# One masked copy per block instead of two in the windowed attention of a two-layer decoder trunk, with the difference of the values as the second operand

## The chip, the cores and the metric

One core of a Trainium2 chip runs the whole program. The metric is the device time of one execution in microseconds (us). Three runs of the kernel before took 986.33, 987.54 and 988.58 us; their median is 987.54 us.

The engines that matter are TensorE (PE in the profile; PEld are its weight loads), VectorE (DVE), ScalarE (ACT), GpSimd (POOL) and SyncE (SP, which issues nearly all DMAs). Each works through its own instructions in program order and waits at an instruction until semaphores of the others allow it.

## The reference

The trunk has two layers over 1024 positions of width 1024. Layer 0 is a gated pooling mixer and isn't touched. Layer 1 is gated attention with 16 heads of width 64, two key/value heads, a sink per head, a position bias, and a window of 128 positions. In blocks of 128 queries it is:

```python
def block_fn(args):
    qn, kn, vn, mn = args            # kn, vn: the previous and the own block, 256 keys
    s = jnp.einsum('bqhgd,bkhd->bhgqk', qn, kn).astype(jnp.float32) + pos_bias
    s = jnp.where(mn[None, None, None], s, NEG_INF)
    m = jnp.maximum(jnp.max(s, axis=-1, keepdims=True), sink)
    p = jnp.exp(s - m)
    p = p / (jnp.sum(p, axis=-1, keepdims=True) + jnp.exp(sink - m))
    return jnp.einsum('bhgqk,bkhd->bqhgd', p.astype(vn.dtype), vn)
...
o = o.transpose(1, 0, 2, 3, 4, 5).reshape(B, S, B_WIDTH)
return (o * jax.nn.silu(z)) @ w_out
```

The mask lets query i of a block see key j of the previous block for j > i, and key j of its own block for j <= i. For a given place j of the 128, a query so sees exactly one of the two keys.

## The kernel before

The activations lie with the channel on the partitions and the positions along a row. Every operand of a matmul is split into a high and a low part, so a product takes three matmuls (L203, L204, L205 in `dense_mm`: weights `wh`, `wl` against both parts of the activations). The weights are loaded by SP into `raw` and split there and then by `split_w` (L121 on ACT, L123 on DVE).

Layer 1 is one list of steps, `specs` (L1332), in two halves `q` of 512 positions. For each half and each of four groups `r` of four heads there are two steps `queries`, then `start`, then two steps `gates`; between them stand `keys`, `values` and `values_split` of the second half, the preparation of the activations of later steps (`Modulated.step`: L177 on DVE, L159 and L163 on ACT, L167 on POOL), and the output projections. `start` puts four blocks `attend(q, r, b)` on a list of events with due times, in units of an estimated PE time; the order of PE is written out by it (`manual_schedule` for PE alone, L1355). The other engines of layer 1 have their instructions ordered by a scheduler of the framework, which is why their order can shift when instructions are added.

One `attend` has three parts. First the scores go into a bank of PSUM (L1097, L1098); since a place j belongs to one key only, the scores of the two blocks are merged there by a predicated copy with the triangle `tri` (L1099), so that a block has 128 scores for a query instead of 256; bias, minimum and exponential follow (L1103 on DVE, L1107 on ACT), then the reciprocal and the scaling (L1110, L1111 on DVE). Some microseconds later PE transposes the probabilities into the bank "tp" (L1117), and ACT and DVE split them into `cur` (L1120, L1121). A `cur` holds probabilities that belong partly to keys of the previous block and partly to keys of the own one. For a block with b > 0, POOL makes the masked copy `prev` (L1126, what belongs to the previous block, the rest zero) and then masks `cur` in place (L1129). After a further pause PE multiplies the values of the previous block by `prev` and those of the own block by `cur` into bank "o" (L1140, L1141, two matmuls each). There are 28 such blocks; the four with b = 0 have no previous block.

Bank "o" exists once. It is emptied by ACT into the tile `ol` (L1143) and by DVE, which adds the two halves (L1147, twice); gate and split follow (L1151, L1152, L1153).

The values come from `values(q)`: ACT copies the projection out of PSUM into the tile `vt` (L1025). `values_split(q)` (L1030) transposes it on PE into a bank "d" (L1034), and splits it there into `VS` (L1037 on ACT, L1038 on DVE): `VS` has for each of 16 slots (block times key/value head) a high and a low part of 64 columns each. `vt` and `ol` share the tag "ol" of the pool `bp`, with one buffer: a new tile of that tag gets it only when every reader of the tile before is done. The first `values_split` stands behind the first `queries` of the half q = 0, the second behind the first `queries` of its third group.

Of the kernel before, what the change touches and what calls it, by code (L numbers as in the profile page):

```python
# [12 lines left out]
F32 = mybir.dt.float32  # L13
F32R = mybir.dt.float32r
AF = mybir.ActivationFunctionType
ALU = mybir.AluOpType
PSUM = bass.MemoryType.PSUM

P = 128
D = 1024  # L20
T = 1024
H = 512
# [33 lines left out]
def trunk(ctx, tc, xT, c, pack, ada_first, ada_rest, wu0_in, wg0_in, wa, wg, wao, wkv,  # L56
          wb, wbo, bias_in, outT):
    nc = tc.nc
# [7 lines left out]
    pp = ctx.enter_context(tc.tile_pool(name="psum", bufs=1, space=PSUM))  # L66
# [3 lines left out]
    def bank(tag):  # L70
        return pp.tile([P, H], F32, tag=tag, name="ps_" + tag, bufs=BANKS[tag])
# [146 lines left out]
    with ExitStack() as sa:  # L218
# [111 lines left out]
        blk, blk_k = {}, {}  # L330
# [467 lines left out]
        with tc.manual_schedule(engines={ET.PE}):  # L798
            nxt = pair_w(*steps[0])
            for i, (kind, g, j) in enumerate(steps):  # L800
                w, nxt = nxt, pair_w(*steps[i + 1]) if i + 1 < len(steps) else None
                if kind == "U":
                    parts = []
# [172 lines left out]
        with tc.manual_schedule(engines={ET.PE, ET.Activation, ET.DVE, ET.Pool}):  # L976
            for _, _, f, args in sorted(plan, key=lambda e: e[:2]):
# [3 lines left out]
    bp = ctx.enter_context(tc.tile_pool(name="bpool", bufs=1))  # L981
# [6 lines left out]
                            channel_multiplier=1, compare_op=ALU.is_ge, fill=0)  # L988
# [2 lines left out]

    VS = bp.tile([P, 16, 2, 64], F32R, name="VS")

# [23 lines left out]
    vts = {}  # L1020
# [9 lines left out]
    def values_split(q):  # L1030
        def run(w):
            ps = bank("d")
            for j in range(4):
                nc.tensor.transpose(ps[:, j * P:(j + 1) * P], vts[q][:, j * P:(j + 1) * P], ident)  # L1034
            pv = ps.rearrange("p (s c) -> p s c", c=64)
            vh, vl = VS[:, q * 8:q * 8 + 8, 0, :], VS[:, q * 8:q * 8 + 8, 1, :]
            nc.scalar.copy(out=vh, in_=pv)  # L1037
            nc.vector.tensor_sub(out=vl, in0=pv, in1=vh.bitcast(F32))  # L1038
            yield 0.43
        return None, run  # L1040

# [36 lines left out]
    def attend(q, r, b):  # L1078
        kv = r // 2
# [6 lines left out]
                              in_=nsink[:, 4 * r:4 * r + 4].unsqueeze(2))  # L1086
        nm = sp.tile([P, 4], F32, tag="nm", name="nm")
        den = sp.tile([P, 4], F32, tag="den", name="den")
        for j in range(2):
            s = bank("S").rearrange("p (e c) -> p e c", e=2)  # L1090
            lo = 0 if b else P
# [8 lines left out]
            for e in range(2):  # L1100
# [3 lines left out]
                    out=pt[:, i, :P], in0=s[:, e, :P], in1=bias[:, hd, :],  # L1104
# [7 lines left out]
                             in1=den.unsqueeze(2).broadcast_to([P, 4, P]))  # L1112
# [6 lines left out]
        cur = bp.tile([P, 2, H], F32R, tag="ph", name="cur", bufs=2)  # L1119
        nc.scalar.copy(out=cur[:, 0], in_=tp)  # L1120
        nc.vector.tensor_sub(out=cur[:, 1], in0=tp, in1=cur[:, 0].bitcast(F32))  # L1121
        parts = [(b, cur)]
        if b:
            prev = bp.tile([P, 2, H], F32R, tag="pp", name="prev", bufs=1)
            v8 = lambda t: t.rearrange("p x (a i) -> p (x a) i", i=P)
            nc.gpsimd.affine_select(out=v8(prev), in_=v8(cur).bitcast(F32),  # L1126
                                    pattern=[[0, 8], [-1, P]], base=-1, channel_multiplier=1,
                                    compare_op=ALU.is_ge, fill=0.0)
            nc.gpsimd.affine_select(out=v8(cur), in_=v8(cur).bitcast(F32),  # L1129
                                    pattern=[[0, 8], [1, P]], base=0, channel_multiplier=-1,  # L1130
                                    compare_op=ALU.is_ge, fill=0.0)
            parts = [(b - 1, prev), (b, cur)]
        yield LAGS[1]
        while (q, r) not in szs:
            yield KSTEP
        sz = szs[q, r]
        o = bank("o")
        for x, (blk, ph) in enumerate(parts):
            v = VS[:, 2 * blk + kv].rearrange("p x c -> p (x c)")
            mm(o, v, ph[:, 0], start=x == 0, stop=False)  # L1140
            mm(o, v, ph[:, 1], start=False, stop=x == len(parts) - 1)  # L1141
        ol = bp.tile([P, H], F32, tag="ol", name="ol", bufs=1)
# [2 lines left out]
        for e in range(2):  # L1145
            es = slice(e * 2 * P, (e + 1) * 2 * P)
            nc.vector.scalar_tensor_tensor(  # L1147
                out=of[e * 64:(e + 1) * 64, :], in0=o[0:64, es], scalar=0.5,
                in1=ol[0:64, es], op0=ALU.mult, op1=ALU.add)
# [4 lines left out]
                             in1=qt[:, :, 0, cols].bitcast(F32))  # L1154
# [132 lines left out]
    def start(q, r, gap):  # L1287
        def f():
            t = max(clock[0] + FIRST, last_start[0] + gap)
            for b in range(4):  # L1290
                push(t + gap * b, attend(q, r, 4 * q + b))
            last_start[0] = t + gap * 3
        return bare(f)
# [130 lines left out]
```

## Time and profile before

The profiled execution took 987.29 us, its span from the first to the last instruction 985.4 us, at a mean granted PE clock of 0.998.

| engine | busy, us | share of the span | instructions |
|---|---|---|---|
| PE | 962.5 | 98% | 4538 |
| DVE | 776.1 | 79% | 1411 |
| ACT | 458.6 | 47% | 902 |
| POOL | 143.8 | 15% | 173 |

Matmuls overlap in the profile: a 128x512 one is shown with about 390 ns, while one starts every 0.22 to 0.23 us. So a busy PE says that it never lacked work, not that it is at its peak, and its real losses are the rows in which it waits. A row of a timeline gives the start, the duration, the engine, the line of the kernel, the operation, output and inputs, and how many instructions are merged; where an engine was idle before, a bracket gives the idle time and the instruction that ended it. A row of the waits gives who waited for whom, the total, the number of times and the longest.

### The profile page before, as it was taken

To read this page: it belongs to the slowest core of one execution; us is meant where nothing else is said; L and a number is where in the kernel's file an instruction comes from. 1 tells how busy PE (TensorE), PEld (TensorE's weight loads), DVE (VectorE), ACT (ScalarE), POOL (GpSimd) and SP (SyncE) were. 2 spreads that over 40 slices of the span, in tenths; PEclk is the share of its full clock that TensorE was granted. 3 is DMA by queue.
4 is the path that set the end of the run, shared out by engine and by line. 5 is a ranking of instruction groups with operands and counts; after the bars stand their busy time and mean duration, and the time that the engine had idled before them with its cause. 6 is when DMAs were issued, how large, how long until landed. Compare 5 with 4: busy or idle time off the path is not lost.

```text
span 985.4 us, 12696 instructions
## 1 busy us (share of the span) xinstructions
PE 962.5 (98%) x4538; PEld 800.6 (81%) x4538; DVE 776.1 (79%) x1411; ACT 458.6 (47%) x902; POOL 143.8 (15%) x173
## 2 busy tenths in 40 slices
PE   8999999999999999999999998999999999999996
PEld 6788888888888887888888886877788888887786
DVE  5997978687978698677772268599899878889995
ACT  6533435333433244551111235486677555656534
POOL 2100000000000000000000000053334213336723
PEclk9999999999999999999999999999999999999999
DMA  9453621254125412789861212312221221123222
GB/s 332 182 171 124 192 91 65 88 190 159 55 99 189 157 48 76 245 300 329 303 200 55 74 64 101 114 65 65 79 71 65 87 86 65 64 85 109 86 87 85
DMA packets 40625, 125.67 MB, mean 128 GB/s; under 512 B 4465, under 2 KB 6641, under 8 KB 40434
## 3 DMA queue, kind: packets, MB, share of 16 engines
q1 hardware_dynamic: 40416, 123.82, 36.8%
q10 hardware_dynamic: 146, 1.05, 0.3%
q8 instruction: 35, 0.57, 0.2%
q14 instruction: 28, 0.23, 0.1%
HBM read 111.22 MB, written 13.63 MB: 127 GB/s over the span
## 4 chain that ended last, share of the span: by engine, by line
PE 73%; DVE 18%; ACT 3%; issue 3%; POOL 1%; DMA 1%; SPq 0%; POOLq 0%; DVEq 0%; ACTq 0%
PE ps_d L214 13%; PE ps_d L635 9%; PE ps_S L214 8%; PE ps_d L205 6%; PE ps_d L203 6%; PE ps_d L204 6%; PE ps_S L635 4%; PE ps_o L214 4%; PE ps_tp L214 3%; DVE wl L123 3%; PE ps_tp L635 2%; PE ps_o L635 2%; DVE tmp L541 2%; PE ps_d L374 2%; PE ps_tp L1117 1%
## 5 line engine op out<-in xcount | busy, mean ns | idle before, releaser
L121 ACT CAST wh<-raw 128x1024 fp32r<-128x1024 f32 x80 | 83.7, 1047 | 110.4 <-PE ps_d L214 78.0
L123 DVE TENSOR_TENSOR wl<-raw,wh 128x1024 fp32r<-128x1024 f32 x80 | 102.8, 1285 | 37.0 <-ACT wh L121 33.1
L203 PE MATMUL ps_d<-hm,wh 128*128 128x512 f32 x288 | 114.0, 396 | 1.1 <-ACT wh L121 1.1
L205 PE MATMUL ps_d<-hm,wl 128*128 128x512 f32 x288 | 112.7, 391 | 1.4 <-DVE wl L123 1.4
L204 PE MATMUL ps_d<-hm,wh 128*128 128x512 f32 x288 | 112.5, 391 | 0.0
L239 DVE CUSTOM_DVE_ANT_0 tmp<-tmp,cact,pk 128x1024 f32<-128x1024 f32 x48 | 60.6, 1282 | 29.6 <-DMA tmp<-ada_rest 29.5
L214 PE MATMUL ps_d<-gh,wh 128*128 128x512 f32 x224 | 82.0, 389 | 0.0
L205 PEld LDWEIGHTS ps_d<-hm,wl 128*128 128x128 f32 x288 | 54.1, 188 | 14.4 <-DVE wl L123 3.0
L214 PE MATMUL ps_S<-gh,wh 128*128 128x512 f32 x192 | 64.5, 390 | 0.0
L203 PEld LDWEIGHTS ps_d<-hm,wh 128*128 128x128 f32 x288 | 54.2, 188 | 11.7 <-ACT wh L121 1.5
L635 PE MATMUL ps_d<-hs,ws 128*128 128x512 f32 x264 | 63.4, 389 | 0.0
L1107 ACT ACTIVATE pt<-pt,nm 128x129 f32<-128x129 f32 x128 | 50.1, 394 | 26.8 <-DVE nm L1103 24.6
L204 PEld LDWEIGHTS ps_d<-hm,wh 128*128 128x128 f32 x288 | 54.2, 188 | 9.9
L635 PEld LDWEIGHTS ps_d<-hs,ws 128*128 128x128 f32 x264 | 49.6, 188 | 10.3
L541 DVE TENSOR_TENSOR tmp<-tmp 128x1039 f32<-128x1039 f32 (+3 forms) x40 | 49.4, 1235 | 6.8 <-ACT tmp L671 5.7
L611 ACT CAST ws<-tw 128x512 fp32r<-128x512 f32 x44 | 26.8, 621 | 54.5 <-PE ps_tp L214 15.1
L635 PE MATMUL ps_d<-ha,ws 128*128 128x512 f32 x216 | 51.9, 389 | 0.0
L533 POOL MEMSET tmp<- 128x16 f32 x16 | 1.7, 111 | 331.0 <-DVE tmp L541 116.2
L214 PEld LDWEIGHTS ps_d<-gh,wh 128*128 128x128 f32 x224 | 42.0, 188 | 8.7
L635 PEld LDWEIGHTS ps_d<-ha,ws 128*128 128x128 f32 x216 | 40.6, 188 | 8.4
L214 PE MATMUL ps_d<-gh,wl 128*128 128x512 f32 x112 | 43.6, 389 | 0.0
L147 POOL TENSOR_TENSOR rs<-v,mhalf 128x4 f32<-128x4 f32 (+1 forms) x7 | 7.1, 1018 | 239.7 <-DVE v L145 239.7
(292 smaller groups left out, 2477.0 us busy)
## 6 DMA issues: line engine op xcount, KB each, us to landing
tmp<-ada_rest SPq DMA_DIRECT2D x48, 512.0 KB, 4.5
raw<-wb SPq DMA_DIRECT2D x32, 512.0 KB, 3.3
raw<-wa SPq DMA_DIRECT2D x28, 512.0 KB, 3.5
raw<-wao SPq DMA_DIRECT2D x20, 512.0 KB, 3.7
ad<-ada_first SPq DMA_DIRECT2D x16, 512.0 KB, 4.9
x<-xT SPq DMA_DIRECT2D x32, 256.0 KB, 5.8
raw<-wbo SPq DMA_DIRECT2D x16, 512.0 KB, 3.3
kept_g<-tmp SPq DMA_DIRECT2D x14, 512.0 KB, 2.9
```

The costliest lines, as they stand in the source:

```text
L121: nc.scalar.copy(out=wh, in_=raw)
L123: nc.vector.tensor_sub(out=wl, in0=raw, in1=wh.bitcast(F32))
L203: mm(ps, lh, acts(k, 0), start=k == 0, stop=False)
L204: mm(ps, lh, acts(k, 1), start=False, stop=False)
L205: mm(ps, ll, acts(k, 0), start=False, stop=k == n - 1)
L214: mm(p, lhs, acts(k, hl, q), start=start and k == 0 and s == 0, stop=stop and k == n - 1 and s == 2)
L239: nc.vector.tensor_tensor_reduce(out=raw, in0=raw, in1=ca, scale=0.5, scalar=pk[:, bcol:bcol + 1], op0=ALU.mult, op1=ALU.add, accum_out=ad ...
L374: mm(psu[i, q], w0[k // 2][:, k % 2, w, i * P:(i + 1) * P], block(k, q)[hl], start=k == 0 and s == 0, stop=k == KT - 1 and s == 2)
L541: nc.vector.tensor_add(out=nx[:, 2 * s - 1:], in0=cur[:, 2 * s - 1:], in1=cur[:, s - 1:PAD + T - s])
L611: nc.scalar.copy(out=ws[i][:, 0, :], in_=src)
L635: mm(ps, lhs, acts(k, hl), start=start and k == 0 and s == 0, stop=k == 3 and s == 2, skip_group_check=True)
L1107: nc.scalar.activation(pt[:, i, :P + 1], pt[:, i, :P + 1], AF.Exp, bias=nm[:, i:i + 1], scale=-1.0, accum_out=den[:, i:i + 1])
```

## The change

`VS` stays. A second tile `DS` holds, in the same layout, the difference of the values: own block minus previous block. A block with b > 0 now multiplies the unmasked probabilities `cur` by the values of the previous block, and one masked copy `own` (what belongs to the own block) by the difference; the sum is the same. `cur` is not masked any more, and the copy `prev` is gone. `values_split` makes `DS`: it copies the transposed values back into `vt` (ACT), subtracts the previous block's values in place in the PSUM bank (DVE), and splits the result (ACT, DVE). The last block of the first half is kept in `v_last` for the second half.

```diff
     VS = bp.tile([P, 16, 2, 64], F32R, name="VS")
 
+    DS = bp.tile([P, 16, 2, 64], F32R, name="DS")
+    v_last = bp.tile([P, 2, 64], F32, name="v_last")
...
             nc.scalar.copy(out=vh, in_=pv)
             nc.vector.tensor_sub(out=vl, in0=pv, in1=vh.bitcast(F32))
+            vf = vts[q].rearrange("p (s c) -> p s c", c=64)
+            nc.scalar.copy(out=vf, in_=pv)
+            lo = 0 if q else 2
+            dh, dl = DS[:, q * 8 + lo:q * 8 + 8, 0, :], DS[:, q * 8 + lo:q * 8 + 8, 1, :]
+            if q:
+                nc.vector.tensor_sub(out=pv[:, 0:2, :], in0=pv[:, 0:2, :], in1=v_last)
+            else:
+                nc.scalar.copy(out=v_last, in_=vf[:, 6:8, :])
+            nc.vector.tensor_sub(out=pv[:, 2:8, :], in0=pv[:, 2:8, :], in1=vf[:, 0:6, :])
+            nc.scalar.copy(out=dh, in_=pv[:, lo:, :])
+            nc.vector.tensor_sub(out=dl, in0=pv[:, lo:, :], in1=dh.bitcast(F32))
             yield 0.43
...
-        parts = [(b, cur)]
+        parts = [(VS, b, cur)]
         if b:
-            prev = bp.tile([P, 2, H], F32R, tag="pp", name="prev", bufs=1)
+            own = bp.tile([P, 2, H], F32R, tag="pp", name="own", bufs=1)
             v8 = lambda t: t.rearrange("p x (a i) -> p (x a) i", i=P)
-            nc.gpsimd.affine_select(out=v8(prev), in_=v8(cur).bitcast(F32),
-                                    pattern=[[0, 8], [-1, P]], base=-1, channel_multiplier=1,
-                                    compare_op=ALU.is_ge, fill=0.0)
-            nc.gpsimd.affine_select(out=v8(cur), in_=v8(cur).bitcast(F32),
+            nc.gpsimd.affine_select(out=v8(own), in_=v8(cur).bitcast(F32),
                                     pattern=[[0, 8], [1, P]], base=0, channel_multiplier=-1,
                                     compare_op=ALU.is_ge, fill=0.0)
-            parts = [(b - 1, prev), (b, cur)]
+            parts = [(VS, b - 1, cur), (DS, b, own)]
...
-        for x, (blk, ph) in enumerate(parts):
-            v = VS[:, 2 * blk + kv].rearrange("p x c -> p (x c)")
+        for x, (vs, blk, ph) in enumerate(parts):
+            v = vs[:, 2 * blk + kv].rearrange("p x c -> p (x c)")
```

Lines behind the insertion have other numbers in the changed kernel; in its rows below L1040 and L1041 are the split into `VS` (L1037, L1038 before), L1043 the copy into `vt`, L1047 and L1050 the subtractions, L1051 and L1052 the split into `DS`, L1068 and L1069 the split of the queries (L1054, L1055), L1121 the exponential (L1107), L1156 `ol` (L1143), L1160 to L1166 the steps behind it (L1147 to L1153), L1142 the masked copy, L1099 the small copy of POOL (L1085).

The order of PE has the same rows at the same places, with `cur` and `own` in place of `prev` and `cur`. The first place that changes otherwise is POOL's, at the first two blocks with b > 0. Before:

```order
L1085 COPY pt<-nsink 128x4
L167 TENSOR_TENSOR hm<-xn,hm 128x512
L1126 AFFINE_SELECT prev<-cur 128x1024
L1129 AFFINE_SELECT cur<-cur 128x1024
L167 TENSOR_TENSOR hm<-xn,hm 128x512 x2
L1085 COPY pt<-nsink 128x4
L1126 AFFINE_SELECT prev<-cur 128x1024
L167 TENSOR_TENSOR hm<-xn,hm 128x512
L1129 AFFINE_SELECT cur<-cur 128x1024
```

Now:

```order
L1099 COPY pt<-nsink 128x4
L167 TENSOR_TENSOR hm<-xn,hm 128x512
L1142 AFFINE_SELECT own<-cur 128x1024
L167 TENSOR_TENSOR hm<-xn,hm 128x512 x2
L1099 COPY pt<-nsink 128x4
L1142 AFFINE_SELECT own<-cur 128x1024
L167 TENSOR_TENSOR hm<-xn,hm 128x512 x3
```

The second masked copy is gone, and L167 follows the first at once. The second place is ACT's, at the second `values_split`. Before:

```order
L1107 ACTIVATE pt,den<-pt,nm 128x129 x3
L1143 ACTIVATE ol<-ps_o 64x512
L1107 ACTIVATE pt,den<-pt,nm 128x129
L1054 ACTIVATE qt<-ps_d 64x512
L1037 CAST VS<-ps_d 128x8x64
L121 CAST wh<-raw 128x1024
L1152 CAST qt<-of 128x2x128
L1054 ACTIVATE qt<-ps_d 64x512
L159 ACTIVATE hm<-xn,adac,acol 128x512 x2
L1143 ACTIVATE ol<-ps_o 64x512
L163 ACTIVATE xn<-xn,adac,acol 128x512
```

Now, with what each instruction waits for (the engine whose semaphore it is):

```order
L1121 ACTIVATE pt,den<-pt,nm 128x129 [waits DVE_49] x3
L1068 ACTIVATE qt<-ps_d 64x512 [waits PE_49]
L1040 CAST VS<-ps_d 128x8x64 [waits PE_49]
L121 CAST wh<-raw 128x1024 [waits DMAHW5_49]
L1068 ACTIVATE qt<-ps_d 64x512 [waits DVE_49]
L1043 COPY vt<-ps_d 128x512 [waits DVE_49]
L159 ACTIVATE hm<-xn,adac,acol 128x512 x2
L163 ACTIVATE xn<-xn,adac,acol 128x512 [waits Activation_49]
L1156 ACTIVATE ol<-ps_o 64x512 [waits DVE_49]
L1051 CAST DS<-ps_d 128x8x64
```

The first of the two `ol` has moved from between the exponentials to behind the copy into `vt`, two L159 and an L163, and waits for DVE. The third place is DVE's at the same point. Now:

```order
L1124 RECIPROCAL den<-den 128x4
L1125 TENSOR_TENSOR pt<-pt,den 128x4x128
L1069 SCALAR_TENSOR_TENSOR qt<-ps_d,qt 64x512
L1041 TENSOR_TENSOR VS<-ps_d,VS 128x8x64
L123 TENSOR_TENSOR wl<-raw,wh 128x1024
L1069 SCALAR_TENSOR_TENSOR qt<-ps_d,qt 64x512
L1047 TENSOR_TENSOR ps_d<-ps_d,v_last 128x128
L1050 TENSOR_TENSOR ps_d<-ps_d,vt 128x384
L1160 SCALAR_TENSOR_TENSOR of<-ps_o,ol 64x256 x2
L1052 TENSOR_TENSOR DS<-ps_d,DS 128x8x64
L1164 TENSOR_TENSOR of<-of,szb 128x256
L177 TENSOR_TENSOR xn<-x,rb_4924 128x512
```

Before, the two L1147 (L1160 here) stood ahead of the reciprocal (L1110, L1124 here); now they stand behind the two subtractions. Two L177 that stood further back in the program now stand among the steps behind them.

## The prediction

> **What bounds the kernel now.** I read the page first for the span, then the waits of TensorE (PE), then the busy time by stretches, then the timelines of the engines where PE waits.
>
> ```profile
> span 985.4 us, 12696 instructions
> ```
>
> The profiled execution took 987.29 us, so 1.9 us lie outside the span. The change touches only layer 1, from about 620 us on. The busy time there, by stretches (start and end; span; then PE, weight load, DVE, ACT and POOL, each with its count):
>
> ```profile
> 640.00:710.00 70.00, 65.86 (x327) 54.32 (x327) 65.76 (x153) 54.24 (x122) 29.29 (x26) 1.00 0.19 61
> 710.00:740.00 30.00, 29.92 (x156) 25.21 (x155) 27.87 (x69) 20.79 (x49) 9.25 (x10) 1.00 0.26 88
> 740.00:900.00 160.00, 160.00 (x799) 135.06 (x798) 136.12 (x345) 95.92 (x238) 51.56 (x54) 1.00 0.23 76
> 900.00:940.00 40.00, 37.20 (x192) 30.46 (x191) 37.71 (x87) 24.05 (x62) 28.77 (x22) 1.00 0.27 92
> ```
>
> From 740 to 900 us PE never pauses: whatever delays PE before that is paid in full, and whatever DVE or POOL save there is worth nothing. PE is idle for 4.1 us in 640 to 710 and for 2.8 us in 900 to 940, the two places where DVE is 94% busy. What it waits for in all of layer 1:
>
> ```profile
> PE ps_tp L1117 <- DVE pt L1111: 6.1, 5, 1.6
> ```
>
> That is the probabilities of a block, the last DVE step before PE transposes them. No row has PE waiting for a masked copy (L1126, L1129). So the removal can earn only through DVE, and at most those 6.1 us and the 0.34 us of L205 below. The places (start, duration; the last bracket is PE's idle time and its releaser), with two rows where it does not wait now:
>
> ```profile
> 659.67 0.63 PE L1117 MATMUL ps_tp<-ident,pt 128*128 128x128 f32 x4 [1.60 <-DVE pt L1111]
> ...
> 694.24 0.60 PE L1034 MATMUL ps_d<-ident,vt 128*128 128x128 f32 x4
> ...
> 698.80 0.39 PE L1140 MATMUL ps_o<-prev,VS 128*128 128x512 f32 x1
> ...
> 708.89 0.50 PE L205 MATMUL ps_d<-hm,wl 128*128 128x512 f32 x1 [0.34 <-DVE wl L123]
> ...
> 903.98 0.63 PE L1117 MATMUL ps_tp<-ident,pt 128*128 128x128 f32 x4 [1.52 <-DVE pt L1111]
> ```
>
> **The change, part by part: what it removes.** PE issues the same matmuls in the same order with other operands, so its own work is unchanged. POOL loses one of two masked copies in 28 blocks (count, total, mean in ns):
>
> ```profile
> L1129 POOL TENSOR_SCALAR_AFFINE_SELECT cur<-cur 128x1024 fp32r<-128x1024 f32 x28 | 32.5, 1160 | 1.8
> ```
>
> 32.5 us of POOL go, but POOL is idle most of the time, and PE reads its copy several us after it is made. What can count is that DVE runs longer while POOL works. POOL, then DVE, at two of the waits:
>
> ```profile
> 655.28 1.16 POOL L1129 TENSOR_SCALAR_AFFINE_SELECT cur<-cur 128x1024 fp32r<-128x1024 f32 x1
> 656.41 1.30 POOL L167 TENSOR_TENSOR hm<-xn,hm 128x512 fp32r<-128x512 f32 x1
> ...
> 899.99 1.09 POOL L1129 TENSOR_SCALAR_AFFINE_SELECT cur<-cur 128x1024 fp32r<-128x1024 f32 x1
> ```
>
> ```profile
> 657.32 0.94 DVE L177 TENSOR_TENSOR xn<-x,rb 128x512 f32<-128x512 f32 x1
> 658.27 0.66 DVE L177 TENSOR_TENSOR xn<-x,rb 128x512 f32<-128x512 f32 x1
> ...
> 900.64 1.52 DVE L123 TENSOR_TENSOR wl<-raw,wh 128x1024 fp32r<-128x1024 f32 x1
> ```
>
> At 657.32 L177 takes 0.94 us instead of the 0.66 of its twin, because L167 holds POOL until 657.71; L167 stood behind the removed copy. Without it, L167 ends about 1.2 us earlier and L177 is free: **0.28 us** sooner for pt, and PE's wait at 659.67 falls from 1.60 to 1.32. At 900.64 L123 takes 1.52 us against 1.23 (row 700.27 below): 0.29 us go, and I take **0.28 us** off the wait at 903.98, with bounds of 0 and 0.36, because a POOL addition that was held up by this L123 can move forward and hold up pt instead. At the other three waits of L1117 either no masked copy lies beside the DVE steps ahead, or another POOL step (L167) holds pt up afterwards anyhow. The first masked copy stays where it was, right behind L1121, so what DVE loses to that one stays too. Together −0.56 us; bounds 0 and −3.0 (half of the 6.1 us, as half of the masked copies go).
>
> [...]
>
> **What it adds.** For each half of the sequence, values_split now copies the transposed values into vt (ACT), subtracts in place in the PSUM bank (one step of DVE for the first half, two for the second), splits the difference (ACT, DVE), and, for the first half, keeps two slots in v_last. The first time it falls at 621 to 626 us, ahead of attention, where ACT idles behind PE's projections:
>
> ```profile
> 626.13 1.05 ACT L121 CAST wh<-raw 128x1024 fp32r<-128x1024 f32 x1 [3.79 <-PE ps_d L204]
> ```
>
> The DVE step that follows (L123) needs this wh, so DVE has the same gap, and I cost the first time at 0; if that cover were gone, at 1.1 us (two DVE steps on 384 columns, by the estimate below).
>
> The second time it stands at 695 us, where DVE has no room. And vt lies in the only buffer of tag "ol". Until now that buffer came free when PE had transposed vt (L1034, over at 694.84); now the last reader is the in-place subtraction on DVE (L1050 of after.py). Behind it waits ol (L1143), the ACT step that starts the evacuation of bank o; behind ol, L1147 on DVE; behind L1147, PE at L1140 of the next block, since bank o exists once. ACT now (first), and DVE now:
>
> ```profile
> 695.12 0.59 ACT L1143 ACTIVATE ol<-ps_o 64x512 f32<-64x512 f32 x1
> 695.62 0.39 ACT L1107 ACTIVATE pt<-pt,nm 128x129 f32<-128x129 f32 x1
> 695.91 0.19 ACT L1107 ACTIVATION_READ_ACCUMULATOR pt<-pt,nm 128x1 f32 x1
> 696.13 0.59 ACT L1054 ACTIVATE qt<-ps_d 64x512 fp32r<-64x512 f32 x1
> 696.63 0.57 ACT L1037 CAST VS<-ps_d 128x512 fp32r<-128x512 f32 x1
> 697.09 1.05 ACT L121 CAST wh<-raw 128x1024 fp32r<-128x1024 f32 x1
> 698.04 0.41 ACT L1152 CAST qt<-of 128x256 fp32r<-128x256 f32 x1
> 698.47 0.59 ACT L1054 ACTIVATE qt<-ps_d 64x512 fp32r<-64x512 f32 x1
> 699.09 1.52 ACT L159 ACTIVATE hm<-xn,adac,acol 128x512 fp32r<-128x512 f32 x2
> 700.51 0.58 ACT L1143 ACTIVATE ol<-ps_o 64x512 f32<-64x512 f32 x1
> 701.00 0.80 ACT L163 ACTIVATE xn<-xn,adac,acol 128x512 f32<-128x512 f32 x1
> ```
>
> ```profile
> 699.55 0.69 DVE L1055 SCALAR_TENSOR_TENSOR qt<-ps_d,qt 64x512 fp32r<-64x512 f32 x1
> 700.27 1.23 DVE L123 TENSOR_TENSOR wl<-raw,wh 128x1024 fp32r<-128x1024 f32 x1
> 701.53 0.85 DVE L1147 SCALAR_TENSOR_TENSOR of<-ps_o,ol 64x256 f32<-64x256 f32 x2
> ```
>
> I lay the new order over these rows, on the clock of before. On ACT the fourth exponential moves up into ol's place, from 695.62 to about 695.05, and its sum is read by 695.55. L1054, L1037, L121 follow at the present distances: 695.6, 696.1, 696.55 to 697.6; the second L1054 ends at 698.2. On DVE the reciprocal starts at 695.6; with 0.2 us for it, 0.6 to 0.7 us for L1111 and 0.72 us for L1055 (699.55 to 700.27), L1038 runs from 697.2 to 697.9, L123 to 699.0, the second L1055 from 699.0 to 699.75. ACT's copy into vt waits for L1038, runs to 698.6, and is not what is late.
>
> The subtractions have no row. The nearest are L1055, from PSUM with 512 columns in 0.69 us, which I use for L1038 as well, and one on PSUM with 256 columns (shortest, median, longest in ns):
>
> ```profile
> L1099 DVE COPY_PREDICATED ps_S<-tri,ps_S x61: 414/423/430, 640.0 to 937.6; 128x256 f32<-128x256 int8 x61
> ```
>
> Half the columns save 0.26 us, so 128 columns take about 0.29 us and 384 about 0.55. Each waits for the one ahead: 699.8 to 700.1, then to 700.65. On ACT the two L159 now run from 698.6 to 700.05 and one L163 (0.80, with 0.72 to the next) ends at 700.8, so ol is free to start at **700.75**, 5.6 us later than at 695.12, and ends at 701.35. L1147 twice, 0.85 us: 702.2. PE starts about 0.05 to 0.15 us later, say 702.3, instead of 698.80: a new wait of **3.5 us**. Bounds: 1.5 us, if the subtractions and handovers ran in the shortest rows' time and the scheduler's position cost nothing (ol right after vt is copied, at 698.6, and the same 1.55 us behind it would end at 700.2); 4.5 us, if a POOL step holds up L123 here by its whole 1.2 us. I take the middle replay since each of its steps is a row.
>
> After it DVE has about 1.5 us more to do (0.55 and 0.29 and the last split of about 0.69), and two L177 that stood further back come among it. But PE is 3.5 us later as well, so the 0.34 us at 708.89 should go: **−0.3 us**; bounds −0.34 and +0.8, if POOL holds up L1151 or L123 there.
>
> Sum: 987.29 + 3.5 − 0.56 − 0.3 = **989.9 us**. The median of the three runs, 987.54, lies 0.25 above the profiled execution, so beside that median I expect 990.1; I write **990.0**.
>
> **The rivals.** *DVE is set free and that decides.* If the copies that go hold DVE up by more than single rows show, the waits on pt and wl vanish, 6.1 + 0.34 us: with the new wait 987.3 − 6.4 + 3.5 = 984.4 us, faster. For it: DVE is the engine that PE waits for in both places, and POOL is over 40% busy in 640 to 710 and 72% in 900 to 940. Against: the copy that stays hits the same DVE steps as before, and I find a removed one ahead of two of the five waits only. It decides as soon as more than 5.5 us go, which takes the 3.5 and the 2 that can be measured. Chance 0.10.
>
> *The new wait does not come.* ol gets its buffer early enough, or bank o is free for another reason; then only the gains stay, 987.3 − 0.9 = 986.4 us, no measurable change. For it: this stands on one order of two engines at one place. Against: ol stands behind the copy and waits for DVE in the changed order. Chance 0.16.
>
> *The debt goes on.* The extra DVE work and the earlier L177 make wl late at 708.89 by more than now, and the next L1117 too: another 1 to 2 us, 991.5 us. Chance 0.12.
>
> *The change doesn't do what it says.* The order has 28 single masked copies, so this has no chance worth a number.
>
> **How the numbers follow.** My forecast has 0.62; its own range is 988.8 to 991.0 us, the new wait between 2.3 and 4.5. About 0.2% (2 us) is what a measurement of this kernel can tell from no change, so slower begins at 989.5. Of the 0.62 I put 0.50 above it, with the 0.12 of the debt: slower 0.62. Same: 0.12 + 0.16 = 0.28. Faster 0.10. The range goes from 986.0 (the median, the shortest new wait and the largest gain: 987.5 + 1.5 − 3.0) to 991.6 (the longest new wait, the smallest gain, and the end of the debt's case); it leaves out the faster rival and a little above, less than 0.2.
>
> **What would show it.** Right: PE's waits get a row of L1140's successor (ps_o) on DVE's of (L1147), one time, 3 to 4 us, at about 699 us; ol starts 5 to 6 us after the value transposes; the row at 659.67 is 0.3 us shorter; 740 to 900 us stays at 100% PE; POOL busy falls by some 32 us and DVE's mean for L123 hardly. Wrong: no such row, or a shorter one than 2 us; waits of L1117 falling by more than 2 us in total; L1117 or L205 waiting longer after 710 us.

## The result, and the profile after

The changed kernel takes **996.55 us** (median of five runs, 995.90 to 996.73), the kernel before 988.58 beside it (five runs, 986.33 to 989.11): a ratio of **1.0082**, with a 95% interval of 1.0069 to 1.0095. It is slower by 8 us. The prediction had the direction, and 990.0 us with a range up to 991.6; so the time is wrong by 6.5 us, of which 1.0 is that the kernel before, too, has a higher median here than at the forecast (988.58 against 987.54). Later, beside other runs of the kernel before, the same kernel gave 1.0083 (1.0070 to 1.0096).

The profiled execution took 995.9 us. Its page begins with the span:

```profile
span 993.2 us, 12687 instructions
```

The span is 7.8 us longer than before; the other 0.8 us lie outside the span, and nothing in the trace says why. The busy time by the stretches that the prediction used (start and end; span; PE, weight load, DVE, ACT, POOL, each with its count; PE's granted clock; DMA share; GB/s):

```profile
640.00:710.00 70.00, 63.06 (x307) 51.93 (x306) 64.98 (x147) 52.38 (x114) 23.48 (x21) 0.95 0.19 61
710.00:740.00 30.00, 27.69 (x141) 23.31 (x140) 22.99 (x61) 17.42 (x44) 2.95 (x5) 1.00 0.22 68
740.00:900.00 160.00, 160.00 (x799) 134.96 (x798) 135.84 (x349) 98.62 (x246) 32.17 (x38) 1.00 0.24 77
900.00:940.00 40.00, 38.46 (x197) 32.11 (x195) 36.55 (x81) 23.62 (x57) 24.46 (x18) 1.00 0.32 105
```

From 740 to 900 us PE still never pauses. All that was lost lies in the first two rows: PE is idle for 6.9 us in 640 to 710 (4.1 before) and for 2.3 us in 710 to 740 (0.1 before), and in the first row its clock is 0.95 where it was 1.00. PE's waits in layer 1:

```profile
PE ps_tp L1131 <- DVE pt L1125: 4.0, 5, 1.2
PE ps_o L1153 <- DVE of L1160: 3.4, 1, 3.4
PE ps_S L1111 <- DVE ps_S L1107: 2.3, 1, 2.3
...
PE ps_d L205 <- DVE wl L123: 1.5, 2, 1.0
```

The second row is the wait that was predicted. The third was not: one set of scores (L1111, L1097 before) waits for the memset of its own bank (L1107, L1093 before). PE's timeline has both, and the waits that became shorter:

```profile
660.15 0.63 PE L1131 MATMUL ps_tp<-ident,pt 128*128 128x128 f32 x4 [1.22 <-DVE pt L1125]
670.20 0.63 PE L1131 MATMUL ps_tp<-ident,pt 128*128 128x128 f32 x4 [0.75 <-DVE pt L1125]
679.35 0.50 PE L205 MATMUL ps_d<-hm,wl 128*128 128x512 f32 x1 [1.01 <-DVE wl L123]
...
703.03 0.77 PE L1153 MATMUL ps_o<-cur,VS 128*128 128x512 f32 x1 [3.41 <-DVE of L1160]
...
720.46 0.30 PE L1111 MATMUL ps_S<-KH,qt 128*128 128x128 f32 x1 [2.31 <-DVE ps_S L1107]
...
911.78 0.63 PE L1131 MATMUL ps_tp<-ident,pt 128*128 128x128 f32 x4 [0.78 <-DVE pt L1125]
```

The matmul at 703.03 is shown with 0.77 us, where its kind took 0.39: a third cost, beside the two waits. In this trace the clock changes at 602.76, 606.17, 701.74 and 708.57 us, that is only at multiples of 3.413 us from its first change; PE's stretches, cut at these places (such a stretch of 3.41 us is called a window below):

```profile
698.33:701.74 3.41, 1.29 (x6) 0.75 (x4) 2.88 (x5) 3.36 (x6) 0.27 (x1) 1.00 0.31 67
701.74:705.16 3.42, 2.13 (x5) 1.77 (x6) 3.07 (x5) 1.72 (x4) 2.27 (x2) 0.50 0.21 86
705.16:708.57 3.41, 3.41 (x12) 2.72 (x12) 2.80 (x7) 1.89 (x4) 0.19 (x1) 0.50 0.00 0
708.57:711.98 3.41, 3.41 (x20) 2.92 (x20) 3.12 (x13) 2.59 (x10) 1.14 (x1) 1.00 0.00 0
```

Read the sixth figure behind the span: in the window with the pause PE works 1.29 of 3.41 us, and for the next two windows its clock is 0.50. In those a 128x512 matmul starts every 0.43 us, where it was 0.23 ahead of the pause; PE works 2.13 + 3.41 = 5.5 us and does the work of 2.8, so **2.7 us** are lost behind the pause. "Half clock" below means such a stretch at 0.50.

The account of the span, from how far the same PE instruction stands behind the kernel before: 0.2 us up to 598 us; 0.7 more at about 603, where this execution also ran 3.4 us at half clock and the profiled one of before did not; −0.3 from 660.15 to 691 us; +3.6 at 703.03; +2.7 up to 708; −0.6 up to 718 (the 0.34 us at 708.89 are gone); +2.5 at 720.46; −0.2 up to 900; −0.7 at 911.78. Sum: 7.9, measured 7.8.

Why is the memset late? Before, DVE did both memsets of that block at once, ahead of the second `wl`:

```profile
710.43 0.55 DVE L1093 MEMSET ps_S<- 128x256 f32 x2
710.88 1.21 DVE L123 TENSOR_TENSOR wl<-raw,wh 128x1024 fp32r<-128x1024 f32 x1
```

Now the second one comes 5 us after the first:

```profile
715.04 0.27 DVE L1107 MEMSET ps_S<- 128x256 f32 x1
715.94 1.23 DVE L123 TENSOR_TENSOR wl<-raw,wh 128x1024 fp32r<-128x1024 f32 x1 [0.63 <-ACT wh L121]
717.20 0.69 DVE L1083 SCALAR_TENSOR_TENSOR szb<-szb,ps_d 128x512 f32<-128x512 f32 x1
...
719.61 0.42 DVE L1113 COPY_PREDICATED ps_S<-tri,ps_S 128x256 f32<-128x256 int8 x1
720.04 0.27 DVE L1107 MEMSET ps_S<- 128x256 f32 x1
```

The scheduler has put a `wl`, a gate, both L1160, L1135, L1164 and the predicated copy L1113 between the two, 15 to 20 us behind the place where steps were added. POOL has become what was announced, with 28 copies less:

```profile
L1142 POOL TENSOR_SCALAR_AFFINE_SELECT own<-cur 128x1024 fp32r<-128x1024 f32 x28 | 32.3, 1154 | 46.9 <-DVE cur L1135 46.9
```

### The profile page after: what moved, and what is told of

It is laid out like the page before. It is cut to its first block, busy times and chain, and to the rows that moved or that the text cites. A ratio compares the mean times of both kernels' runs of the same rounds, so it can differ in the third digit from the quotient of the medians.

```text
span 993.2 us, 12687 instructions
## 1 busy us (share of the span) xinstructions
PE 966.5 (97%) x4538; PEld 803.8 (81%) x4538; DVE 775.6 (78%) x1416; ACT 461.1 (46%) x907; POOL 109.6 (11%) x145
## 3 DMA queue, kind: packets, MB, share of 16 engines
q10 hardware_dynamic: 146, 1.05, 0.3%
## 4 chain that ended last, share of the span: by engine, by line
PE 76%; DVE 17%; ACT 3%; issue 2%; DMA 1%; POOL 1%; SPq 0%; POOLq 0%; DVEq 0%; ACTq 0%
PE ps_d L214 13%; PE ps_d L635 9%; PE ps_S L214 8%; PE ps_d L203 7%; PE ps_d L205 7%; PE ps_d L204 7%; PE ps_S L635 4%; PE ps_o L214 4%; PE ps_tp L214 3%; DVE wl L123 2%; PE ps_o L635 2%; PE ps_tp L635 2%; DVE tmp L541 2%; PE ps_d L374 2%; PE ps_tp L1131 1%
## 5 line engine op out<-in xcount | busy, mean ns | idle before, releaser
L123 DVE TENSOR_TENSOR wl<-raw,wh 128x1024 fp32r<-128x1024 f32 x80 | 100.0, 1249 | 38.7 <-ACT wh L121 34.8
L1121 ACT ACTIVATE pt<-pt,nm 128x129 f32<-128x129 f32 x128 | 50.2, 395 | 27.2 <-DVE nm L1117 24.9
L214 PEld LDWEIGHTS ps_S<-gh,wh 128*128 128x128 f32 x192 | 35.9, 188 | 7.3
```

Source lines behind the costliest of these rows:

```text
L123: nc.vector.tensor_sub(out=wl, in0=raw, in1=wh.bitcast(F32))
L214: mm(p, lhs, acts(k, hl, q), start=start and k == 0 and s == 0, stop=stop and k == n - 1 and s == 2)
L1121: nc.scalar.activation(pt[:, i, :P + 1], pt[:, i, :P + 1], AF.Exp, bias=nm[:, i:i + 1], scale=-1.0, accum_out=den[:, i:i + 1])
```

## Experiments

Three questions were open: whether the three costs (wait, half clock, memset) each stand alone; what the removed copies are worth by themselves; and whether the work that the change adds costs because of what it is or because of where it stands. A table first; the pauses are PE's waits from 690 to 725 us in the profiled execution, named by what PE waits for (pt: the probabilities, L1125; wl: the low part of the weights, L123; o: bank o; memset: that of the scores' bank), and the half clock is the time at a granted clock of 0.50 behind them.

| kernel | pauses, us | half clock, us | profiled, us | median, us | ratio to before, 95% interval |
|---|---|---|---|---|---|
| before | pt 0.56, wl 0.34 | 0 | 987.29 | 988.45 to 989.23 | |
| changed | pt 0.55, o 3.41, memset 2.31 | 6.8 | 995.9 | 996.55 | 1.0082 (1.0069 to 1.0095) |
| own_tile | pt 0.54, wl 1.51, memset 2.86 | 0 | 991.34 | 995.67 | 1.0058 (1.0041 to 1.0074) |
| memset | pt 0.56, o 3.40, wl 0.41 | 0 | 991.49 | 992.64 | 1.0031 (1.0020 to 1.0042) |
| both | pt 0.56, wl 2.08 | 3.4 | 992.29 | 992.54 | 1.0035 (1.0022 to 1.0048) |
| select_only | pt 0.55 | 0 | 987.35 | 987.38 | 0.9977 (0.9968 to 0.9986) |
| ds_only | pt 0.54, o 3.39, memset 2.32 | 6.8 | 995.3 | 997.08 | 1.0083 (1.0069 to 1.0096) |
| hold3 | pt 0.54, o 1.74 | 0 | 991.34 | 991.05 | 1.0022 (1.0011 to 1.0034) |
| pool_ds2 | pt 0.56, wl 2.88 | 3.4 | 990.82 | 992.37 | 1.0038 (1.0025 to 1.0050) |
| filler | pt 0.56, o 1.16, memset 3.26 | 3.4 | 995.75 | 995.67 | 1.0067 (1.0051 to 1.0083) |
| after_b | pt 0.55, o 3.40, memset 2.31 | 3.4 and 3.4 | 997.07 | 997.07 | 1.0083 (1.0070 to 1.0096) |
| late_ds2 | pt 0.54 | 0 | 988.41 | 988.41 | 0.9994 (0.9984 to 1.0005) |

A median holds half clocks elsewhere too, which come and go between executions (the mean clock of 16 runs of the kernel before lies between 0.992 and 0.998); so the pauses are compared in the traces, the times by the ratios.

**own_tile.** The copy gets a buffer of its own, so that vt's is free after the transposes:

```diff
-            vf = vts[q].rearrange("p (s c) -> p s c", c=64)
+            vft = bp.tile([P, H], F32, tag="vf", name="vf", bufs=1)
+            vf = vft.rearrange("p (s c) -> p s c", c=64)
```

> The changed kernel, with the copy vf in a buffer of its own instead of vt's. Theory A (three prices that stand one behind the other: the wait for bank o 3.5 us, the half clock behind it 2.7 us, the late memset 2.3 us): vt's buffer comes free at the transposes again, the wait of 3.41 us for the step of L1160 goes, and with it the half clock; the scheduler also puts both memsets of that block side by side again, so the 2.3 us can go too. Time 996.5 - 8.5 = 988.0 us, TensorE clock 1.00 from 700 to 710 us; 990.3 if the memset still comes late. Theory B (the extra work of ACT and DVE at 695 to 720 us is the cost, and the waits are only where it comes out): the work is the same, so TensorE pauses at pt, wl or the memset instead, 993 to 996 us.

PE's timeline of it:

```profile
710.75 0.50 PE L205 MATMUL ps_d<-hm,wl 128*128 128x512 f32 x1 [1.51 <-DVE wl L123]
716.16 0.30 PE L1112 MATMUL ps_S<-KH,qt 128*128 128x128 f32 x1 [2.86 <-DVE ps_S L1108]
```

The wait for bank o is gone, so the buffer was its cause. But 4.4 us of pauses stand at wl and at the memset in its place, and the runs lie between 991.3 and 997.9; the profiled one is the fastest. Theory A falls as a sum of three separate prices; theory B, that DVE's debt comes out at the next place, has the better of it here (median 995.67, inside its 993 to 996). (The two memsets do stand together in this kernel, but behind all the steps, not ahead of them.)

**memset**, and the same kernel a second time, **memset_b**:

```diff
             if b == 0:
-                nc.vector.memset(s[:, :, :P], NEG)
+                with tc.high_priority():
+                    nc.vector.memset(s[:, :, :P], NEG)
```

> The changed kernel, with the memset of the scores' bank put ahead in the order; the buffer of vt stays shared. Theory A: the pause of 2.31 us at 718.1 us goes and nothing else: 996.5 - 2.3 = 994.2 us; the 3.41 us for bank o and the clock of 0.50 behind it stay. Theory B: DVE has the same work there, so the next wait for pt or wl grows by as much: 996 us.

> The kernel with the memset ahead once more, for a second profile: in the first, the pause of 3.40 us was cut by the grid into 1.62 and 1.77 us and no half clock followed. Theory A: cut otherwise, one part is over 1.9 us and PEclk 0.50 follows for 3.4 or 6.8 us; 1.7 to 3 us more than the first profile's 991.5. Rival: no half clock again.

The memset's pause is gone, and the wait for bank o is unchanged: 3.40 us, and 3.42 in memset_b. Only 0.4 us came back at wl. (At 672 us, where the edit moves another pair of memsets, a wait of 0.75 and one of 1.0 became one of 2.15.) So this pause was a matter of the order alone. The median came out at 992.64 us, below the 994.2 of theory A. The surprise is the clock. Windows of memset on its own grid, at the wait for bank o (none of the windows behind it has a clock under 1.00):

```profile
698.69:702.10 3.41, 1.79 (x8) 1.13 (x6) 3.31 (x5) 3.36 (x6) 0.00 (x0) 1.00 0.17 55
702.10:705.51 3.41, 1.64 (x7) 1.38 (x8) 2.63 (x5) 2.02 (x4) 2.53 (x2) 1.00 0.25 99
```

The same pause as in the changed kernel, cut by the grid into 1.62 and 1.77 us, costs no clock. memset_b was to show another cut and did not: 1.64 and 1.78, again without half clock. It did show one at 673 us, behind a window that was idle for 1.96 us, and took 993.42 us in its one run:

```profile
669.95:673.36 3.41, 1.45 (x7) 0.87 (x5) 3.36 (x6) 3.27 (x7) 2.18 (x2) 1.00 0.18 41
673.36:676.77 3.41, 3.21 (x13) 2.95 (x13) 3.37 (x6) 1.82 (x3) 1.60 (x2) 0.50 0.30 118
```

**both** has the two edits together.

> The changed kernel with both edits: own buffer for vf, memset ahead. Theory A: neither pause nor half clock; 988.0 us, the same as with the buffer alone if its memset is in time, 2.3 us less if not. Theory B: 993 to 996 us.

Neither the wait for bank o nor the memset's is left, yet PE waits once more for wl, and the half clock follows:

```profile
712.86 0.50 PE L205 MATMUL ps_d<-hm,wl 128*128 128x512 f32 x1 [2.08 <-DVE wl L123]
```

With 0.9 us of waits here before, it is 1.7 us more. DVE got 1.6 us of steps (L1047, L1050, L1052; rows further down). So what is left when buffer and order are mended is about the added work of DVE itself. Both theories missed the time; A by 4.5 us, B by 0.5.

**select_only** is the removing half alone: the kernel before with one masked copy, and VS instead of DS as second operand. It leaves out the differences, so it computes something else than the trunk and shows only what the removed copies are worth in time.

```diff
-            nc.gpsimd.affine_select(out=v8(prev), in_=v8(cur).bitcast(F32),
-                                    pattern=[[0, 8], [-1, P]], base=-1, channel_multiplier=1,
-                                    compare_op=ALU.is_ge, fill=0.0)
-            nc.gpsimd.affine_select(out=v8(cur), in_=v8(cur).bitcast(F32),
+            nc.gpsimd.affine_select(out=v8(own), in_=v8(cur).bitcast(F32),
...
-            parts = [(b - 1, prev), (b, cur)]
+            parts = [(b - 1, cur), (b, own)]
```

> The kernel before, with the first block's probabilities used unmasked and one masked copy a block as in the change, but with the values and not their difference for the own block: this leaves out the making of the difference, so the output isn't the reference's. The order of TensorE, DVE, ACT and SP is that of before; only GpSimd has 28 copies less. Theory A (copies that go are worth what single rows show: 0.3 to 0.9 us at 660, 0.7 us at 904, part of it given back): 987.0 to 988.0 us against 988.6. The rival (GpSimd holds DVE up and decides): the waits for pt and wl go, 982 to 984 us. A further rival, nothing: 988.6.

PE's waits in its timeline (lines as before, since nothing is inserted ahead):

```profile
660.71 0.63 PE L1117 MATMUL ps_tp<-ident,pt 128*128 128x128 f32 x4 [1.36 <-DVE pt L1111]
670.76 0.63 PE L1117 MATMUL ps_tp<-ident,pt 128*128 128x128 f32 x4 [0.74 <-DVE pt L1111]
679.93 0.50 PE L205 MATMUL ps_d<-hm,wl 128*128 128x512 f32 x1 [1.05 <-DVE wl L123]
...
903.64 0.63 PE L1117 MATMUL ps_tp<-ident,pt 128*128 128x128 f32 x4 [0.78 <-DVE pt L1111]
```

The removal gains: −0.24, −0.91, +1.05, −0.34 (the wait at 708.89, gone) and −0.74 are −1.2 us of pauses; the ratio says 0.14 to 0.32%, 1.4 to 3.2 us. The rival of a large gain through DVE is out. DVE as a whole is busy for 772.0 us, 4.1 less than before.

**ds_only** is the adding half alone: the kernel before, with `DS` made by the same lines and not used.

> The kernel before, with both masked copies a block kept and the differences DS made as in the change but not used: the adding half of the change alone. The order of DVE and ACT at 695 to 720 us is that of the change, with the late second memset. Theory A2 (what was found so far: the buffer's wait of 3.4 us, the half clock behind it, then the work that is added to DVE comes out at wl, pt or the memset, 2 to 3 us; the copies that go give 1.9 us): 989 + 3.4 + 2.7 + 2.5 = 997 to 998.5 us, with the row of bank o on the successor of L1147 at 3.3 to 3.6 us. Rival (the change is slow because the single masked copy or the operands of the matmuls are): 989 to 991 us.

Its PE timeline has the two pauses of the changed kernel to 0.02 us:

```profile
702.14 0.77 PE L1153 MATMUL ps_o<-prev,VS 128*128 128x512 f32 x1 [3.39 <-DVE of L1160]
...
719.70 0.30 PE L1110 MATMUL ps_S<-KH,qt 128*128 128x128 f32 x1 [2.32 <-DVE ps_S L1106]
```

The whole loss comes from making `DS`, with both masked copies and the old operands in place. This profile is the clean account: like before's it has no half clock at 603 us, and its span of 993.58 is 8.15 longer: 3.39 + 2.32 + 2.7 (6.8 us at half clock, less the part in which PE waited) − 0.34 = 8.1.

**hold3** is the held buffer alone: in the kernel before, three transfers read `vt` one behind the other after the second transposes, and no engine but SP gets work.

```diff
+            if q:
+                sc = bp.tile([P, H], F32, name="sc")
+                nc.sync.dma_start(sc, vts[q])
+                nc.sync.dma_start(sc, vts[q])
+                nc.sync.dma_start(sc, vts[q])
             yield 0.43
```

> The kernel before, with no difference made, but with vt's buffer held by three DMA copies, one behind the other, of vt into a scratch tile, second half only: no engine gets work but SyncE issues three transfers. ol then stands behind the next copies on ACT as in the change, and the memsets stay side by side. Theory A (buffer alone makes the pause, and a pause of over about 2 us inside one 3.41 us window halves the clock for the next window): TensorE waits 2.5 to 5 us for the step of L1147 at about 700 us, behind it PEclk 0.50 for 3.4 or 6.8 us; 989 + 3.5 + 1.7 to 3.4 = 994 to 996 us. Rival (without more work on DVE and ACT the held buffer is caught up): under 1 us of pause, 989 to 990 us.

```profile
702.36 0.47 PE L1145 MATMUL ps_o<-prev,VS 128*128 128x512 f32 x1 [1.74 <-DVE of L1152]
```

PE waits 1.74 us, less than expected, with no half clock behind it and the memsets side by side: 1.0022 (1.0011 to 1.0034), about 2.2 us. A later release of that buffer is enough to make PE wait for bank o, and this pause cost only itself: PE's clock is 1.00 from 690 to 722 us.

**pool_ds2** takes the three causes out: own buffer, differences made on POOL, the memset of the group r = 2 ahead.

```diff
-                nc.vector.tensor_sub(out=pv[:, 0:2, :], in0=pv[:, 0:2, :], in1=v_last)
+                nc.gpsimd.tensor_sub(out=df[:, 0:2, :], in0=vf[:, 0:2, :], in1=v_last)
...
-            nc.vector.tensor_sub(out=pv[:, 2:8, :], in0=pv[:, 2:8, :], in1=vf[:, 0:6, :])
-            nc.scalar.copy(out=dh, in_=pv[:, lo:, :])
-            nc.vector.tensor_sub(out=dl, in0=pv[:, lo:, :], in1=dh.bitcast(F32))
+            nc.gpsimd.tensor_sub(out=df[:, 2:8, :], in0=vf[:, 2:8, :], in1=vf[:, 0:6, :])
+            nc.scalar.copy(out=dh, in_=df[:, lo:, :])
+            nc.gpsimd.tensor_sub(out=dl, in0=df[:, lo:, :], in1=dh.bitcast(F32))
```

> The change with the three causes taken out: vf in a buffer of its own, the differences and their low parts made on GpSimd from vf (DVE gets no step more, the PSUM bank is not written), and the memset of the third group's first block put ahead. Theory A2: the time of the single masked copy alone, 987 to 988 us, below before (989.2). Rival (GpSimd's steps at 699 to 706 us hold up hm or the DVE steps beside them as much as DVE's own did): wl or pt wait 1.5 to 3 us at 705 to 720 us, 990 to 992 us.

The rival was right in what it named; the median of 992.37 us lies just above its 990 to 992. DVE and PE:

```profile
703.68 0.69 DVE L177 TENSOR_TENSOR xn<-x,rb 128x512 f32<-128x512 f32 x1 [2.60 <-POOL hm L167]
```

```profile
711.03 0.50 PE L205 MATMUL ps_d<-hm,wl 128*128 128x512 f32 x1 [2.88 <-DVE wl L123]
```

POOL's new steps hold up L167, an L177 that the scheduler moved forward waits 2.6 us for it at the head of DVE's queue, and the wl behind it is late. Another engine at the same place was no cure here.

**filler** adds work to the changed kernel: ten matmuls that nobody reads, into a free bank "d", right ahead of the block that waits for bank o. The other engines keep their order.

```diff
+        if (q, r, b) == (0, 1, 1):
+            fd = bank("d")
+            for i in range(10):
+                mm(fd, VS[:, kv].rearrange("p x c -> p (x c)"), cur[:, 0], start=True, stop=True)
         o = bank("o")
```

> The changed kernel with ten matmuls more, whose result nobody reads, put ahead of the block that waits for bank o at 699.6 to 703.0 us; the order of every other engine is the same to the row. Theory A (TensorE's clock is halved for the next 3.41 us when one window of a grid of 3.41 us was idle for about 1.6 to 2.1 us or more): the ten take 10 x 0.227 = 2.3 us out of the pause, which ends at the same time; no window is idle for more than 1.2 us, no row of PEclk 0.50 stands behind it, and the kernel with more work is faster by the 2.7 us that the half clock took: 996.5 - 2.7 = 993.8 us. Rival (the half clock has another cause, such as the load, or comes by the length of the wait): PEclk 0.50 stays, 996.5 us or 2 us more.

**after_b** is the changed kernel once more, beside filler on the same chip.

> The changed kernel once more, beside the others of this call. Theory A: 996 to 997 us in most runs; the pause of 3.4 us lies at another place of the grid, and the half clock behind it lasts 3.41 or 6.83 us, or does not come where the pause is cut about in half. Rival (the half clock belongs to the program): 6.83 us behind that pause, as in the first profile.

Windows of after_b on its grid:

```profile
700.93:704.34 3.41, 0.30 (x1) 0.30 (x2) 2.56 (x6) 3.36 (x6) 1.26 (x1) 1.00 0.45 154
704.34:707.76 3.42, 3.42 (x12) 2.75 (x11) 3.42 (x6) 1.00 (x2) 1.28 (x1) 0.50 0.00 0
...
718.00:721.41 3.41, 1.10 (x8) 0.93 (x7) 3.36 (x12) 0.96 (x3) 1.15 (x1) 1.00 0.47 154
721.41:724.82 3.41, 3.41 (x9) 2.64 (x8) 1.88 (x9) 1.63 (x8) 0.00 (x0) 0.50 0.03 5
```

Here the grid lies otherwise, the first half clock lasts one window instead of two, and the memset's pause, which cost no clock in the first profile (there it was cut into 0.66 and 1.65 us), has one too. In filler, PE restarts as early as in after_b (11.7 us behind the pt wait at about 692 us in both), having worked through two thirds of the pause, and the clock stays:

```profile
702.00:704.00 2.00, 0.84 (x4) 0.48 (x3) 1.47 (x4) 1.75 (x3) 1.33 (x2) 1.00 0.38 152
704.00:706.00 2.00, 2.00 (x12) 1.69 (x11) 2.00 (x4) 0.51 (x2) 1.28 (x2) 1.00 0.00 0
706.00:708.00 2.00, 2.00 (x14) 1.79 (x14) 1.96 (x6) 1.98 (x4) 0.09 (x1) 1.00 0.00 0
```

This isn't luck with the grid: filler's has a boundary at 702.32, so without the ten matmuls the pause, from about 700.1 to 703.48, would have left about 2.2 us idle in one window, and 1.96 were enough elsewhere (memset_b). So it is PE's idling that decided here: with 1.15 us idle in that window the clock stayed at 1.00, with 3.11 us in after_b's it went to 0.50. The time won is only half kept: PE then waits 3.26 us for the memset instead of 2.31, since DVE is no faster, and this pause fills one window (0.15 us busy of 3.41), and the clock of the next is 0.50. The median is 1.4 us below after_b's, not the 2.7 expected, and the intervals of the two overlap.

**late_ds2** moves the work instead: the differences are made from `VS` (both parts, in SBUF), three steps on POOL, one copy on ACT, one more on POOL, for the second half only behind a masked copy of a later block. `vt` and the PSUM bank are not written.

```diff
+    def values_diff(q):
+        def f():
+            lo, hi = 8 * q + (0 if q else 2), 8 * q + 8
+            h = lambda t, a, b, x: t[:, a:b, x, :].bitcast(F32)
+            d = bp.tile([P, 2, 8, 64], F32, tag="df", name="df", bufs=1)[:, :, :hi - lo, :]
+            for x in range(2):
+                with tc.issue_after(sel[0]) if q else ExitStack():
+                    nc.gpsimd.tensor_sub(out=d[:, x], in0=h(VS, lo, hi, x),
+                                         in1=h(VS, lo - 2, hi - 2, x))
+            nc.gpsimd.tensor_add(out=d[:, 0], in0=d[:, 0], in1=d[:, 1])
+            nc.scalar.copy(out=DS[:, lo:hi, 0, :], in_=d[:, 0])
+            nc.gpsimd.tensor_sub(out=DS[:, lo:hi, 1, :], in0=d[:, 0], in1=h(DS, lo, hi, 0))
+        return bare(f)
...
+        values_diff(1),
         *project(1, 0, h11, GAPS[4]),
```

> The change with the differences made from VS, on GpSimd with one copy on ACT, and for the second half only at 750 to 770 us, where TensorE never waits; vt is not written, nothing is added at 690 to 720 us, and the order of DVE is that of before to the row. Theory A2 (the adding half costs because of where it stands): the gain of the single masked copy is left, 987.0 to 987.8 us against 989, with no wait for bank o, pt or wl at 697 to 725 us. Rival (GpSimd's steps there hold up DVE and masked copies, and 740 to 900 us is no longer without a pause): 989 to 991 us.

Its stretches:

```profile
710.00:740.00 30.00, 30.00 (x157) 25.40 (x156) 27.72 (x70) 21.29 (x51) 6.80 (x8) 1.00 0.28 89
740.00:900.00 160.00, 160.00 (x798) 134.97 (x797) 135.72 (x346) 96.48 (x240) 39.61 (x42) 1.00 0.23 77
```

The work lies at 769 to 776 us, where PE never pauses, and 690 to 740 us is as good as before. Beside after_b on the same chip it is 8.7 us faster. Against the kernel before it is 0.9994 (0.9984 to 1.0005): no difference that can be told, though its pauses are those of select_only but for one (at 632 us PE waits 0.60 us for the queries, 0.27 before). So no run shows a version with the same result that beats the kernel before. Of the 1.0 us between the medians of select_only and late_ds2, measured on different occasions, the profiled executions, 1.06 us apart too, show this: PE's last matmuls start at 978.64 and 978.71 us, and the rest of the difference lies behind them, where the program only finishes and writes its output. Whether the other executions differ there as well stays open.

## Why the prediction was right and wrong, point by point

**The new wait: right, to a tenth.** The replay gave the two subtractions at 699.8 to 700.65, `ol` at 700.75 and PE's restart at 702.3 on the clock of before. The rows of DVE and ACT after, which stand 0.66 us later there:

```profile
700.40 0.30 DVE L1047 TENSOR_TENSOR ps_d<-ps_d,v_last 128x128 f32<-128x128 f32 x1
700.74 0.57 DVE L1050 TENSOR_TENSOR ps_d<-ps_d,vt 128x384 f32<-128x384 f32 x1
...
702.92 0.69 DVE L1052 TENSOR_TENSOR DS<-ps_d,DS 128x512 fp32r<-128x512 f32 x1
```

```profile
701.42 0.59 ACT L1156 ACTIVATE ol<-ps_o 64x512 f32<-64x512 f32 x1
```

Less 0.66: 699.7 to 700.65, 700.76, and 702.4 for PE. The estimates of 0.29 and 0.55 us for the subtractions were measured as 0.30 and 0.57. own_tile and hold3 show the shared buffer to be the cause. The longest wait of 4.5 us in the range was an estimate that no run shows: POOL did not hold up L123 there, which took 1.22 us (1.23 before).

**The step that failed** is the sum behind it: "987.29 + 3.5 − 0.56 − 0.3" prices a pause of PE at its own length, and ends the story of DVE at 708.89 with "about 1.5 us more to do". Two terms are missing, put at nothing without a reason. One is the half clock behind the pause, 2.7 us in the profile, of which filler shows the cause. The other is the second memset of the scores, 2.3 us, whose order had moved 15 us behind the insertion; the order of DVE showed it before any run, but the replay ended at 702 us and took the rest of the order as unchanged. memset shows that it is a matter of order alone. Together they are 5.0 of the 6.0 us between the 989.9 of that sum and the profiled 995.9. The rest is mainly 0.9 us that PE stands behind by 612 us and 0.8 us outside the span, in neither of which the change has work, less 0.9 us by which the gains were larger than predicted.

**The rival "the debt goes on"** had a chance of 0.12 and 1 to 2 us at wl or the next L1117. It was the right kind, at another row. own_tile and both show what it is: with the buffer free, PE waits 1.5 to 2.1 us for wl, about as much as DVE got of steps (0.30 + 0.57 + 0.69 us).

**The removed copies: right in size, by other rows.** Predicted −0.56 and −0.3; alone (select_only) −1.2 in pauses. The wait at 659.67 fell by 0.24 (0.38 in the changed kernel), the one at 903.98 by 0.74 instead of 0.28: L123 ahead of it takes 1.20 us instead of 1.52, as predicted, and DVE has come forward against PE before that. At 670.63 nothing was predicted, because an L167 would hold pt up anyhow. That reading was wrong: the copy gone, L123 takes 1.22 us instead of 1.68, and L1111 0.67 instead of 1.35, since L167 comes later too. The wait fell by 0.9, and 1.0 came back at 679, at wl. The costliest line of DVE before and after:

```profile
L123 DVE TENSOR_TENSOR wl<-raw,wh 128x1024 fp32r<-128x1024 f32 x80 | 102.8, 1285 | 37.0 <-ACT wh L121 33.1 <-PE ps_o L1141 1.7 <-issue 1.4
```

```profile
L123 DVE TENSOR_TENSOR wl<-raw,wh 128x1024 fp32r<-128x1024 f32 x80 | 100.0, 1249 | 38.7 <-ACT wh L121 34.8 <-PE ps_o L1154 1.7 <-issue 1.4
```

32 us of POOL went, and this line gained 2.8 us: 0.1 us for each copy that is gone (0.15 over all of DVE, by the 4.1 us of select_only, an eighth of the 32.5 us).

**The first `values_split`, costed at 0: right.** In ds_only PE stands 0.2 us ahead of before at 602 us and 0.2 us ahead at 659 us. **The stretch 740 to 900** stayed without a pause, as said.

## What to carry to other kernels

A pause of the bound engine is not paid by its length alone: look what its clock does behind it; the same 3.4 us were cheaper where the grid cut them in two (no half clock in memset, 6.8 us in the first profile). Before adding steps on a busy engine, follow its new order to the next place where the bound engine has slack, not only to the first wait; what a scheduler moves far behind can cost as much as what it moves at once (2.3 us here, against 3.4). And work that only has to be done some time belongs in a stretch where the bound engine never waits: with the differences made at 695 us the kernel is 8 us slower than before, made there on another engine (own buffer, memset ahead) 4 us, and made at 770 us it is level with the kernel before.

## What the hardware showed unasked

The half clock of PE came in whole windows of 3.41 us on a grid: in the traces of before, changed (the first profile), filler, after_b, memset_b and late_ds2, laid out in windows from 590 to 900 us, every stretch at 0.50 (before has none there) began on it and lasted 3.41 us, the one in the first profile behind the wait for bank o 6.83. Where the grid lies in the span differs from execution to execution (2.0 us behind a multiple of 3.413 in the first profile, 1.2 in after_b). It isn't independent of the program's progress, though: the boundary nearest to the end of the wait for wl at 602 to 604 us stood 0.3 us ahead of it in before (the grid by its one change, at 981.10 us), and 0.1, 0.4, 0.7 and 1.1 us behind it in the first profile, late_ds2, memset_b and after_b. From 640 to 900 us five windows of these traces that were at full clock were idle for 1.96 us or more (1.96 in memset_b, 2.12 in the first profile, 2.31 and 3.11 in after_b, 3.26 in filler), and half clock followed each. Windows at full clock that were idle for 1.60 (before), 1.62 and 1.77 (memset), 1.64 and 1.78 (memset_b) and 1.65 us (the first profile) were followed by full clock. At about 603 us, where two waits of 1.1 and 0.5 us fall together, 1.59 to 1.64 us in one window were enough in four traces (first profile, filler, memset_b, late_ds2), and 1.58 were not in after_b; so idle time alone does not give the exact threshold, and what else counts stays open. A pause of 3.4 us cost 0, 3.41 and 6.83 us of half clock in memset, after_b and the first profile, by where the grid cut it. That fits how far runs of one kernel lie apart: of own_tile's, the fastest has 991.34 us at a mean clock of 0.996 and the slowest 997.94 us at 0.989.
